# A two-layer decoder on one core: the second token half's FFN pairs multiplied in one pass over both parts of x, and norm factors spread through DRAM

## The chip, the cores and the metric

One NeuronCore of a Trainium2 chip runs the whole kernel. Work is shared by TensorE (PE, matmuls; PEld is its weight load), VectorE (DVE), ScalarE (ACT), GpSimd (POOL) and SyncE (SP, which only issues DMAs). The metric is the device time of one execution in microseconds; a kernel's time is the median of its runs.

## What is computed

512 tokens of 1024 channels go through two layers, all in fp32:

```
layer 0: h += conv_module(rmsnorm(h))        # pointwise+GLU, causal depthwise conv of 31 taps,
                                             # LayerNorm, swish, pointwise
         h += (silu(x@w_gate) * (x@w_up)) @ w_down,   x = rmsnorm(h)     # FFN, inner width 2816
K, V  =  rmsnorm(h) @ w_kv                   # 4 KV heads of 64
layer 1: q = rmsnorm(h) @ w_q                # 16 heads, window of 128 keys, sinks, T5 bias
         h += attention(q, K, V) @ w_o
         h += FFN(rmsnorm(h))
out   =  rmsnorm(h)
rmsnorm(x, g) = x * rsqrt(mean(x*x) + 1e-6) * g
```

## The kernel before, in words

**Layout.** Channels lie on the 128 partitions and tokens along the free axis, so `h` is eight tiles of 128 x 512. A matmul product is 128 x 128 weights (stationary) by 128 x 512 tokens, or by 256 tokens where a half of the tokens is worked on at a time. The convolution module and the first part of layer 0's FFN (inner pairs 0 to 5) run on token half 0, then on token half 1; everything from the second FFN part on runs on all 512 tokens, except the very end, which goes by halves again.

**Split products.** To keep fp32 accuracy, weights and activations are split into a rounded part `hi` (an ACT copy, L203, L382, L386) and a remainder `lo` (a DVE subtraction, L204, L383, L387). `mm3` (L258 to L264) then issues three matmuls for each product into the same sum: `whi` by `xhi` (L262), `whi` by `xlo` (L263) and `wlo` by `xhi` (L264). Each has its own weight load. `Act` (L266) holds the hi and lo parts of an activation in separate tiles of the pool `quads` (11 buffers).

**Weights.** `PLAN` lists every chunk of 512 KB in the order of use. `get` takes the next; `advance` keeps SP loading `raw` tiles up to six chunks ahead (L187, four buffers) and ACT and DVE splitting three chunks ahead (L203, L204; four buffers of each part). An up chunk holds 8 products of 128 x 128 weights, and so does a down chunk.

**FFN.** `ffn_up` works pair by pair (a pair is 256 inner columns): four chunks per pair, two halves of the channels by gate and up. `evac` (L455) takes the sums of a pair out of PSUM: for 256 tokens L461 multiplies the gate by the norm factors on DVE, L463 is Silu, L464 the product with up, L386 and L387 the split into `hid`. There a pair's gate sums share one PSUM bank and its up sums another. `ffn_part` then multiplies `hid` by the down chunks in two groups of four output tiles; L440 and L441 apply the norm factors and add to `h`. For 512 tokens each of a pair's four sums has a bank, and lines L469 to L473 take them out.

**Norms.** `Rms` sums squares: for each tile of `h` a square on ACT (L336) and an addition on POOL (L340). `step1` forms column sums on PE (L350), their mean on DVE (L352), the power -1/2 on POOL (L354) and a diagonal matrix of the factors (on DVE at L357 for 512 tokens, on ACT at L362 for 256). `spread` (L375) multiplies that by ones to bring the factors to all partitions, `step2` copies them to SBUF (L369). `Next.on_h` (L511) issues split (L382, L383) and square for each tile of `h` as it is finished: `n0` and `n1` are the two token halves' norms before layer 0's FFN, and later ones serve K, V and query, and layer 1's FFN. With 256 tokens the first pair calls `step1` at its end, and its sums are taken out in the middle of the second pair.

**The convolution of half 1** runs on DVE (L611), ACT (L603) and POOL (L604) in the background of half 0's matmuls. `job` and `due_at` hand out its steps at points counted in chunks.

**Attention.** A `unit` is four heads by 128 queries, in four stages (`yield` ends one): scores on PE (L927) and bias with maximum on DVE (L930); exponentials on ACT (L937) and the scaling on POOL (L941); transposes on PE (L948) with their split (L951, L952); the product with V on PE (L960) with its split (L966, L967). `pipeline` advances units three, two, one and no steps old, in that order, once per step; 8 units make a pass, two passes are run. The steps are interleaved with the matmuls of the query and the output projection, and `drain` runs what is left of a pass.

**The end.** `Fin` does the last down chunks and the final norm for token half 0 (`fa`), then half 1 (`fb`). `rows` adds to `h` (L1043), squares on ACT (L1047) and sums squares on POOL (L1049); the last squares of half 1 go straight into small matmuls (L1035). `sums` gives the factors (L1066, L1068, L1070), `spread` brings them to a PSUM bank (L1080) and copies that for POOL (L1082). `out_dve` (L1095) makes most output tiles from the bank, `out_pool` (L1089) the others from the copy.

Tile's scheduler orders each engine's instructions from this program order by its own simulation of their times, and adds all waits; `tc.issue_after` pins an order.

Of the kernel before, what the change touches and what calls it, by code (L numbers as in the profile page):

```python
# [149 lines left out]
def hybrid_trunk(ctx: ExitStack, tc: tile.TileContext, xT, W, prm_in, wdw_in, sinks, relb, onehot, outT):  # L150
# [124 lines left out]


# [50 lines left out]
    class Rms:  # L327
        def __init__(self, bc, tok=ALL):
            self.acc = None
            self.bc, self.tok, self.w = bc, tok, tok.stop - tok.start  # L330
            self.eng = nc.gpsimd
            self.stage = 0
# [10 lines left out]
        def step1(self):  # L343
            if self.stage:
                return
            self.stage = 1
            n = self.w // P
            st = bank()
            for i in range(n):
                nc.tensor.matmul(st[:, i:i + 1], self.acc[:, i * P:(i + 1) * P], ones_c, start=i == 0, stop=i == n - 1)  # L350
            ms = small.tile([P, 4], F32, tag="ms", name=uid("ms"))
            nc.vector.tensor_scalar(ms[:, 0:n], st[:, 0:n], 1.0 / D, EPS, op0=ALU.mult, op1=ALU.add)  # L352
            self.rs = small.tile([P, 4], F32, tag="rs", name=uid("rs"))
            nc.gpsimd.tensor_tensor(self.rs[:, 0:n], ms[:, 0:n], mhalf[:, 0:n], op=ALU.pow)  # L354
            self.diag = temp()[:, 0:self.w]
            if n == 4:
                nc.vector.tensor_mul(self.diag.rearrange("p (n q) -> p n q", n=n),  # L357
                                     ident.unsqueeze(1).to_broadcast([P, n, P]),
                                     self.rs.unsqueeze(2).to_broadcast([P, n, P]))
            else:  # L360
                for i in range(n):
                    nc.scalar.mul(self.diag[:, i * P:(i + 1) * P], ident, self.rs[:, i:i + 1])  # L362
# [60 lines left out]
    def ffn_part(layer, part, xg, tok, rms, on_h=None):  # L423
        lo, hi = (HALVES0, HALVES1)[layer][part]
        hid = ffn_up(layer, lo, hi, xg, tok, rms)
        w = tok.stop - tok.start
        for g in range(2):
            if w == 256:
# [22 lines left out]
    def ffn_up(layer, lo, hi, xg, tok, rms):  # L451
        w = tok.stop - tok.start
        hid = Act(2 * (hi - lo), w)

        def evac(pair, banks):  # L455
            rs_bc = rms.step2()
            if w == 256:
# [18 lines left out]
        for pair in range(lo, hi):  # L476
            if w == 256:
# [4 lines left out]
            for half in range(2):  # L482
                for which in range(2):
# [4 lines left out]
                    for k, m in order:  # L488
                        sl = slice(m * P, (m + 1) * P)
                        mm3(banks[which * 2 + m], (whi[:, k, sl], wlo[:, k, sl]), cut(xg[half * 4 + k], tok),  # L490
                            half == 0 and k == 0 and opens(m, w), half == 1 and k == 3 and closes(m, w))
                    if half == 0 and which == 1:
                        if w == 512:
# [4 lines left out]
            if w == 256 and pair == lo:  # L498
# [6 lines left out]
    class Next:  # L505
        def __init__(self, gains, x=None, bc=None, tok=ALL):
            self.gains, self.tok = gains, tok
# [3 lines left out]
        def on_h(self, i):  # L511
            if self.x is None:
                self.x = {self.gains[0]: Act(KT)}
            if self.rms is None:
                self.bc = new_bc() if self.bc is None else self.bc
                self.rms = Rms(self.bc, self.tok)
# [31 lines left out]
    with tc.tile_pool(name="conv", bufs=2) as cv:  # L548
# [275 lines left out]
        x0 = {"ffn0": Act(KT)}  # L824
        bc0 = new_bc()
        n0 = Next(("ffn0",), x0, bc0, HALF[0])
# [19 lines left out]
    ffn_part(0, 0, x0["ffn0"], HALF[1], n1.rms)  # L846
# [11 lines left out]
    if True:  # L858
# [52 lines left out]
        def unit(gp, jp, n):  # L911
# [6 lines left out]
            sc = at.tile([P, 4, 1 + BAND], F32, tag="sc", name=uid("sc"))  # L918
# [21 lines left out]
            for j in range(4):  # L940
                nc.gpsimd.tensor_scalar(sc[:, j, 1:1 + w], sc[:, j, 1:1 + w], sm[:, j:j + 1], 0.0,  # L941
                                        op0=ALU.mult, op1=ALU.add)
            yield
# [72 lines left out]
    class Fin:  # L1016
        def __init__(self, hf):
            self.hf, self.tok = hf, HALF[hf]
            self.banks, self.hg = [bank() for _ in range(4)], []
            self.n_pool = 2 + hf  # L1020
# [17 lines left out]
        def rows(self, g, other=lambda n, ins: None):  # L1038

            n_add = 4 if self.hf else KT  # L1040
            for i in range(g * 4, g * 4 + 4):
# [5 lines left out]
                nc.scalar.square(sq, t)  # L1047
# [30 lines left out]
        def spread(self):  # L1078
            self.pb = bank()[:, 0:256]
            nc.tensor.matmul(self.pb, ones_m, self.diag, start=True, stop=True)  # L1080
            self.bc = temp()[:, 0:256]
            nc.scalar.copy(self.bc, self.pb)  # L1082
# [32 lines left out]
    for n, (kp, g) in enumerate(steps):  # L1115
# [6 lines left out]
        elif n == 3:  # L1122
            fb.rows(1, fill)
    fa.out_pool()
# [31 lines left out]
```

## Time and profile before

| | |
|---|---|
| timed runs | 1122.11, 1123.65, 1123.83 us; median 1123.65 |
| profiled execution | 1122.53 us, span 1120.7 us, granted clock 0.994 |
| PE busy | 1103.7 us (98%), 6140 matmuls |
| DVE, ACT, POOL busy | 663.5 (59%), 509.2 (45%), 324.0 us (29%) |
| DMA | 128.16 MB, 114 GB/s on average |

The stages of the span, by the stretches used below: to about 150 us the convolution module; 150 to 285 the first FFN part on token half 0, with the convolution of half 1 behind it; to 302 half 1's second pointwise product; to 407 the first FFN part on half 1; to 570 the second FFN part; to 594 K and V; to 724 query, attention and the first output products; from about 757 layer 1's FFN; from 1100 the end.

A row of a stretch has: length, then for PE, PEld, DVE, ACT and POOL the busy time and the count, then PE's granted clock, the DMA share and GB/s. A row of a timeline has start, duration, engine, line, operation, tiles and count, and in brackets how long the engine had been idle and what ended that. A row of groups has busy time and mean duration in ns, then idle time before. A row of waits has who waited for whom: us in total, times, the longest. A row of DMA issues ends in the us from issue to landing. Matmul durations overlap, so the pitch of a stream is read from starts.

### The profile page before, as it was taken

The page shows a single profiled execution, that of the slowest core. Times are in us where ns is not written, and L with a number is a line of the kernel's source. Part 1 is how long each engine was busy: PE and PEld are TensorE (multiplying, and loading weights), DVE is VectorE, ACT ScalarE, POOL GpSimd, SP SyncE. Part 2 cuts the span into 40 slices and gives each one's busy share as a digit, 9 for nine tenths or more (in the row PEclk, how much of TensorE's full clock was granted, in tenths as well). Part 3 has the DMA queues.
Part 4 walks back from the last instruction along what each step waited for, and adds up shares of the span by engine and source line. Part 5 has one row for each costly group of instructions (what it writes and reads, how often), then busy time and mean ns, then how long its engine had stood idle before and what let it go on. Part 6 is the DMA issues. An engine that isn't in the chain of part 4 may idle for free.

```text
span 1120.7 us, 16124 instructions
## 1 busy us (share of the span) xinstructions
PE 1103.7 (98%) x6140; PEld 963.7 (86%) x6140; DVE 663.5 (59%) x1072; ACT 509.2 (45%) x898; POOL 324.0 (29%) x425
## 2 busy tenths in 40 slices
PE   9999998999999999999999999999999999999997
PEld 8888888999999998888888777888888888888886
DVE  4999996977756544533575585674443433444455
ACT  3887787746544322323343564553332211232233
POOL 3999699810200001211230232241111100110014
PEclk9999999999999999999999999999999999999998
DMA  9227054585555542233232111123323232333322
GB/s 357 103 31 83 28 179 133 166 266 177 182 180 181 185 151 95 93 113 94 94 94 93 59 38 39 38 76 98 100 87 110 94 94 94 99 103 100 94 94 76
DMA packets 41722, 128.16 MB, mean 114 GB/s; under 512 B 4491, under 2 KB 12844, under 8 KB 41644
## 3 DMA queue, kind: packets, MB, share of 16 engines
q1 hardware_dynamic: 40924, 126.56, 36.4%
q8 instruction: 48, 0.79, 0.3%
q10 hardware_dynamic: 720, 0.57, 0.2%
q14 instruction: 30, 0.25, 0.1%
HBM read 121.87 MB, written 5.24 MB: 113 GB/s over the span
## 4 chain that ended last, share of the span: by engine, by line
PE 90%; DVE 3%; ACT 3%; issue 2%; POOL 1%; DMA 1%; POOLq 0%; SPq 0%; ACTq 0%; DVEq 0%
PE bank L262 26%; PE bank L263 26%; PE bank L264 25%; PE bank L562 9%; PE bank L927 1%; PE bank L649 1%; PE bank L948 1%; ACT pr L603 1%; POOL pr L604 1%; DVE quad L383 1%; ACT whi L203 1%; DVE wlo L204 0%; DVE bank L611 0%; DVE sc L930 0%; DMA raw<-in_W_dram 0%
## 5 line engine op out<-in xcount | busy, mean ns | idle before, releaser
L263 PE MATMUL bank<-quad,whi 128*128 128x512 f32 (+1 forms) x1584 | 543.6, 343 | 1.7 <-DVE quad L383 1.7
L262 PE MATMUL bank<-quad,whi 128*128 128x512 f32 (+1 forms) x1584 | 543.8, 345 | 0.2
L264 PE MATMUL bank<-quad,wlo 128*128 128x512 f32 (+1 forms) x1584 | 542.9, 343 | 0.0
L204 DVE TENSOR_TENSOR wlo<-raw,whi 128x1024 fp32r<-128x1024 f32 x200 | 269.3, 1347 | 318.2 <-ACT whi L203 310.1
L203 ACT CAST whi<-raw 128x1024 fp32r<-128x1024 f32 x200 | 209.4, 1048 | 355.1 <-PE bank L263 301.2
L263 PEld LDWEIGHTS bank<-quad,whi 128*128 128x128 f32 x1584 | 301.0, 190 | 37.5 <-DVE quad L383 2.8
L262 PEld LDWEIGHTS bank<-quad,whi 128*128 128x128 f32 x1584 | 300.7, 190 | 36.5 <-ACT quad L966 0.6
L264 PEld LDWEIGHTS bank<-quad,wlo 128*128 128x128 f32 x1584 | 300.9, 190 | 34.5 <-DVE wlo L204 0.2
L472 POOL TENSOR_TENSOR tmp<-tmp,tmp 128x512 f32<-128x512 f32 x32 | 45.6, 1425 | 485.1 <-DVE tmp L471 471.5
L604 POOL TENSOR_TENSOR pr<-pr,pr 128x256 f32<-128x256 f32 x208 | 160.5, 822 | 11.0 <-ACT pr L603 11.0
L562 PE MATMUL bank<-quad,w 128*128 128x256 f32 x512 | 114.7, 384 | 0.7 <-DMA w<-in_W_dram 0.7
L611 DVE SCALAR_TENSOR_TENSOR bank<-apad,wdw,bank 128x256 f32<-128x256 f32 x248 | 113.2, 485 | 3.5
L562 PEld LDWEIGHTS bank<-quad,w 128*128 128x128 f32 x512 | 98.5, 193 | 14.9 <-DVE quad L537 0.9
L603 ACT ACTIVATE pr<-apad,wdw 128x256 f32<-128x256 f32 x208 | 99.6, 503 | 23.8 <-POOL pr L604 21.7
L340 POOL TENSOR_TENSOR tmp<-tmp,tmp 128x256 f32<-128x256 f32 (+1 forms) x42 | 45.2, 1076 | 135.2 <-ACT tmp L336 111.1
L470 ACT ACTIVATE tmp<-tmp 128x512 f32<-128x512 f32 x32 | 20.1, 632 | 86.5 <-DVE tmp L469 86.5
L941 POOL TENSOR_SCALAR sc<-sc,sm 128x256 f32<-128x256 f32 (+1 forms) x64 | 30.7, 500 | 86.8 <-DVE sm L939 86.7
L386 ACT CAST quad<-tmp 128x512 fp32r<-128x512 f32 (+1 forms) x48 | 27.8, 584 | 28.9 <-POOL tmp L472 25.0
L471 DVE TENSOR_TENSOR tmp<-bank,rsbc 128x512 f32<-128x512 f32 x32 | 22.1, 691 | 30.1 <-PE bank L264 30.1
L383 DVE SCALAR_TENSOR_TENSOR quad<-h,prm,quad 128x512 fp32r<-128x512 f32 (+1 forms) x40 | 39.4, 1020 | 0.5 <-ACT quad L382 0.4
L937 ACT ACTIVATE sc<-sc,m 128x257 f32<-128x257 f32 (+1 forms) x64 | 30.2, 475 | 15.0 <-DVE m L930 14.8
L387 DVE TENSOR_TENSOR quad<-tmp,quad 128x512 fp32r<-128x512 f32 (+1 forms) x48 | 31.0, 651 | 2.3 <-ACT quad L386 2.3
(137 smaller groups left out, 748.6 us busy)
## 6 DMA issues: line engine op xcount, KB each, us to landing
raw<-in_W_dram SPq DMA_DIRECT2D x208, 512.0 KB, 3.5
w<-in_W_dram SPq DMA_DIRECT2D x15, 512.0 KB, 9.7
fd<-fs SPq DMA_DIRECT2D x1, 3072.0 KB, 33.8
h<-in_xT_dram SPq DMA_DIRECT2D x8, 256.0 KB, 6.3
bias<-fd SPq DMA_DIRECT2D x8, 256.0 KB, 7.2
out_dram<-res SPq DMA_DIRECT2D x13, 128.0 KB, 1.8
w<-in_W_dram SPq DMA_DIRECT2D x2, 256.0 KB, 4.3
out_dram<-res ACTq DMA_DIRECT2D x3, 128.0 KB, 2.4
```

The source lines that it names most:

```text
L203: nc.scalar.copy(hi, r)
L204: lo_engine[0].tensor_sub(lo, r, f32(hi))
L262: nc.tensor.matmul(out, w[0], x[0], start=start, stop=False)
L263: nc.tensor.matmul(out, w[0], x[1], start=False, stop=False)
L264: nc.tensor.matmul(out, w[1], x[0], start=False, stop=stop)
L340: self.eng.tensor_add(sq, self.acc, sq)
L383: nc.vector.scalar_tensor_tensor(dst[1], src, g, f32(dst[0]), op0=ALU.mult, op1=ALU.subtract)
L472: nc.gpsimd.tensor_mul(t2, t1, t2)
L562: mm = nc.tensor.matmul(self.pb[:, w * W2:(w + 1) * W2], w1[ct][:, w, k, :], x[k] if x else xg[k][:, tok], start=k == 0, stop=k == KT - 1)
L603: on_act = nc.scalar.mul(pr, a[:, j:j + W2], tap(j))
L604: on_pool = nc.gpsimd.tensor_add(pr, acc, pr)
L611: on_dve = nc.vector.scalar_tensor_tensor(yt if i == nd - 1 else c, src, tap(i), c if i else self.shift, op0=ALU.mult, op1=ALU.add)
```

## The change

It has five parts.

- **Pairs.** `x0` and half 1's `hid` become `Pairs`: hi and lo parts of a tile lie side by side in one tile. With `twin` (half 1's first FFN part only) `mm2` replaces `mm3`: `whi` by both parts at once, 512 columns into a whole bank (the second half of the bank collects `whi` by `lo`), then `wlo` by `hi`, 256 columns, into the first half. `evac` and `ffn_part` add the two halves of each bank (a copy on ACT, an addition on DVE); products go to POOL. Four banks per pair instead of two. `step1` is called in the middle of the first pair, and that pair's sums are taken out at its end.
- **Norm factors by way of DRAM.** With `by_dma` (`n1` and the two norms for 512 tokens) the factors are written to a DRAM line by SP's queue and read back to all partitions by SP's queue. No diagonal, spread or copy.
- **Norm squares on DVE.** `n0` adds its squares on DVE instead of POOL.
- **Later transposes.** A unit waits one step more between scaling and transposes; score buffers are three.
- **Two spreads.** `fb` spreads its factors into two banks, one for DVE, one for the copy that POOL uses; `fa`'s copy is issued behind `fb`'s last square; `fb` sums five squares on POOL and sends three to PE (four and four before); two tiles of `fb` instead of three go to POOL.

In the diff the first `if twin:` stands in `ffn_part`'s loop over the two groups, the second in `evac`, and the doubled `yield` behind a unit's scaling.

```diff
+    class Pairs:
+        def __init__(self, n, w=512):
+            self.per = 1024 // w
+            self.q = [quads.tile([P, self.per, 2, w], F32R, tag="quad", name=uid("quad")) for _ in range(-(-n // self.per))]
+        def both(self, i):
+            return self.q[i // self.per][:, i % self.per]
+        def __getitem__(self, i):
+            b = self.both(i)
+            return b[:, 0, :], b[:, 1, :]
+
+    def mm2(out, w, x, start, stop):
+        first, second = (w[0], x, out), (w[1], x[:, 0, :], out[:, 0, :])
+        if stop:
+            first, second = second, first
+        nc.tensor.matmul(first[2], first[0], first[1], start=start, stop=False)
+        nc.tensor.matmul(second[2], second[0], second[1], start=False, stop=stop)
...
+            if self.by_dma:
+                line = dpool.tile([1, self.w], F32, tag=uid("line"), name=uid("line"))
+                nc.sync.dma_start(line.rearrange("a (n p) -> p (a n)", p=P), self.rs[:, 0:n])
+                nc.sync.dma_start(self.bc[:, self.tok], line.to_broadcast([P, self.w]))
+                self.stage = 2
+                return
...
+            if twin:
...
+                        mm2(banks[m], (whi[:, k, sl], wlo[:, k, sl]), hid.both(2 * (kp - lo) + k),
+                            kp == lo and k == 0, kp == hi - 1 and k == 1)
+                rs_bc = rms.step2()
+                for m, b in enumerate(banks):
+                    t, hm = temp()[:, 0:w], h[g * 4 + m][:, tok]
+                    nc.scalar.copy(t, b[:, 1, :])
+                    nc.vector.tensor_add(t, b[:, 0, :], t)
+                    nc.gpsimd.tensor_mul(t, t, rs_bc)
+                    nc.vector.tensor_add(hm, hm, t)
+                continue
...
+            if twin:
+                t1, t2 = temp(), temp()
+                for which, t in enumerate((t1, t2)):
+                    for m in range(2):
+                        b = banks[which * 2 + m]
+                        tm = t[:, m * w:(m + 1) * w]
+                        nc.scalar.copy(tm, b[:, 1, :])
+                        nc.vector.tensor_add(tm, b[:, 0, :], tm)
+                t1v, t2v = (t.rearrange("p (a s) -> p a s", a=2) for t in (t1, t2))
+                nc.gpsimd.tensor_mul(t1v, t1v, rs_bc.unsqueeze(1).to_broadcast([P, 2, w]))
+                nc.scalar.activation(t1, t1, AF.Silu)
+                nc.gpsimd.tensor_mul(t2, t1, t2)
+                i = 2 * (pair - lo)
+                q = hid.q[i // 4][:, i % 4:i % 4 + 2]
+                nc.scalar.copy(q[:, :, 0, :], t2v)
+                nc.vector.tensor_sub(q[:, :, 1, :], t2v, f32(q[:, :, 0, :]))
+                return
...
-                        if w == 512:
+                        if w == 512 or twin:
                             rms.step1()
...
-        x0 = {"ffn0": Act(KT)}
+        x0 = {"ffn0": Pairs(KT)}
-        n0 = Next(("ffn0",), x0, bc0, HALF[0])
+        n0 = Next(("ffn0",), x0, bc0, HALF[0], nc.vector, by_dma=False)
...
-    ffn_part(0, 0, x0["ffn0"], HALF[1], n1.rms)
+    ffn_part(0, 0, x0["ffn0"], HALF[1], n1.rms, twin=True)
...
             yield
+            yield
...
-            for t in range(len(units) + 3):
-                for d in (3, 2, 1, 0):
+            for t in range(len(units) + 4):
+                for d in (4, 3, 1, 0):
                     if 0 <= t - d < len(units):
                         next(units[t - d])
+                        if d == 1:
+                            next(units[t - d])
...
-            self.n_pool = 2 + hf
+            self.n_pool = 2
-            n_add = 4 if self.hf else KT
+            n_add = 5 if self.hf else KT
...
             nc.tensor.matmul(self.pb, ones_m, self.diag, start=True, stop=True)
+            if self.hf:
+                pb = bank()[:, 0:256]
+                nc.tensor.matmul(pb, ones_m, self.diag, start=True, stop=True)
+                self.copy(pb)
...
+    with tc.issue_after(fb.squared):
+        fa.copy(fa.pb)
     fa.out_pool()
     fb.sums(fill)
     fb.spread()
```

More of the change, by code (lines that the diff above doesn't have):

```diff
@@ L476, in ffn_up @@
         for pair in range(lo, hi):
-            if w == 256:
+            if twin:
+                full = banks = [bank().rearrange("p (a s) -> p a s", a=2) for _ in range(4)]
+            elif w == 256:
                 full = [bank(), bank()]
@@ L489, in ffn_up @@
                         sl = slice(m * P, (m + 1) * P)
+                        if twin:
+                            mm2(banks[which * 2 + m], (whi[:, k, sl], wlo[:, k, sl]), xg.both(half * 4 + k)[:, :, tok],
+                                half == 0 and k == 0, half == 1 and k == 3)
+                            continue
                         mm3(banks[which * 2 + m], (whi[:, k, sl], wlo[:, k, sl]), cut(xg[half * 4 + k], tok),
@@ L497, in ffn_up @@
                         pending = []
-            if w == 256 and pair == lo:
+            if w == 256 and pair == lo and not twin:
                 rms.step1()
@@ L917, in unit @@
             heads = [gp * 8 + g * 4 + 2 * jp + e for g in range(2) for e in range(2)]
[L918 removed]
+            sc = at.tile([P, 4, 1 + BAND], F32, tag="sc", name=uid("sc"), bufs=3)
             sinks4 = sk.rearrange("p (a g j e) -> p a g j e", a=2, g=2, j=2)[:, gp, :, jp, :]
```

40 lines of the change are left out of this document (22 added, 18 removed).

## Prediction

> **What bounds the kernel now.** I read the page's chain first, then stretches of the span, then pitch of matmuls, then PE's waits.
>
> ```profile
> PE 90%; DVE 3%; ACT 3%; issue 2%; POOL 1%; DMA 1%; POOLq 0%; SPq 0%; ACTq 0%; DVEq 0%
> ```
> ```profile
> 320.00:400.00 80.00, 80.00 (x669) 80.00 (x668) 48.25 (x50) 35.24 (x41) 0.00 (x0) 1.00 0.57 185
> 770.00:1100.00 330.00, 330.00 (x1515) 275.73 (x1514) 143.80 (x153) 96.55 (x119) 34.63 (x26) 1.00 0.30 94
> ```
> ```profile
> 168.00:178.60 10.60, 6.64 (x50) 5.83 (x48) 6.45 (x6) 6.91 (x14) 10.60 (x13) 1.00 0.35 112
> 178.60:183.30 4.70, 4.70 (x27) 4.70 (x28) 1.92 (x3) 3.35 (x6) 4.70 (x6) 0.64 0.51 154
> 656.00:671.00 15.00, 13.02 (x90) 10.51 (x90) 12.06 (x33) 9.70 (x29) 6.76 (x14) 1.00 0.12 37
> 711.00:724.00 13.00, 12.23 (x86) 10.11 (x85) 10.17 (x32) 9.19 (x28) 5.68 (x13) 1.00 0.13 42
> ```
> ```profile
> PE bank L350 <- POOL tmp L340: 3.1, 1, 3.1
> PE bank L263 <- DVE quad L383: 1.7, 4, 0.9
> PE bank L263 <- DVE ptl L952: 1.3, 2, 0.7
> PE bank L262 <- ACT pth L951: 0.6, 1, 0.6
> PE bank L948 <- POOL sc L941: 0.6, 1, 0.6
> ```
>
> TensorE carries 90% of the chain. In the long stretches it is busy every microsecond at clock 1.00 (the first figure of a row is the length, then PE, weight loads, DVE, ACT, POOL, clock), while DVE and ACT have 40% and more to spare. So a matmul taken out there shortens the kernel by its pitch, and work added on DVE, ACT or POOL is free until its queue is late. Outside them TensorE is idle 4.0 us of 168 to 178.6, runs the next 4.7 us at clock 0.64, and idles 2.0 and 0.8 us in the attention's two drains. The waits name who is late. The change touches all these places.
>
> **A. The second half's pairs.** The pitch is the distance between starts:
>
> ```profile
> 339.81 0.28 PE L263 MATMUL bank<-quad,whi 128*128 128x256 f32 x1
> ...
> 345.93 0.28 PE L263 MATMUL bank<-quad,whi 128*128 128x256 f32 x1
> ```
> ```profile
> 469.78 0.39 PE L263 MATMUL bank<-quad,whi 128*128 128x512 f32 x1
> ...
> 475.90 0.39 PE L263 MATMUL bank<-quad,whi 128*128 128x512 f32 x1
> ```
>
> The first pair of rows has 51 steps between them, 120.0 ns each; the second 27, 226.7 ns. Doubling the columns adds 106.7 ns, so about 13.3 ns of each matmul do not depend on columns. The second half's FFN has 6 pairs x 4 chunks x 8 products in up and 2 groups x 6 chunks x 8 in down: 288 products, each of three 256-column matmuls now, one of 512 and one of 256 after. 288 x (3 x 120.0 - 226.7 - 120.0) = **3.8 us**. Not shown is a moving operand in two runs (hi and lo parts lie apart): it could pay the constant twice, and A would be 0. I take 3.8, the pitch of the 512 row.
>
> What it adds: per pair four ACT copies and four DVE additions of 256 from PSUM, the elementwise products moved to POOL. Rows for such work:
>
> ```profile
> L638 DVE TENSOR_TENSOR y<-y,bank 128x256 f32<-128x256 f32 x8 | 3.2, 416 | 1.0 <-POOL y L615 1.0
> L1082 ACT COPY tmp<-bank 128x256 f32<-128x256 f32 x2 | 0.7, 373 | 1.3 <-PE bank L1080 1.3
> L472 POOL TENSOR_TENSOR tmp<-tmp,tmp 128x512 f32<-128x512 f32 x32 | 45.6, 1425 | 485.1 <-DVE tmp L471 471.5
> L203 ACT CAST whi<-raw 128x1024 fp32r<-128x1024 f32 x35 | 36.6, 1047 | 53.1 <-PE bank L263 39.5 <-issue 11.9 <-ACT whi L203 1.0
> ```
>
> 4 x 0.37 = 1.5 us more on ACT and, with two 512 products gone, some 0.3 more on DVE, in a pair of about 11.1 us; POOL gets 2 x 1.43 and has nothing else there. All four PSUM banks of a pair are freed by the copies and additions, without the norm factor, and the next pair has the other four. Cover: casts wait for PE (39.5 us), not PE for casts. Without it the 1.5 us would show in each of six pairs.
>
> The page TensorE: Matmul & The Clock Gate of the Trainium skill ("Back-to-back issue gap") gives an isolated warm matmul its columns at 2.4 per ns plus 2.5 ns; an estimate by that is 288 x 2.5 ns, 0.7 us for A instead of 3.8 and 3.1 us more in the end. The trace disagrees for this stream, with 13.3.
>
> **B. Norm factors by way of DRAM.** For three norms the spread matmul goes (the chain of work in order of time):
>
> ```profile
> 319.63 0.43 PE bank L375 x2
> 588.35 0.86 PE bank L375 x2
> 769.21 0.86 PE bank L375 x2
> ```
>
> 0.43 + 0.86 + 0.86 = **2.1 us**, all in stretches where PE is the bound. Also gone are the diagonal products and copies, off the path. Instead SP issues a write of 256 or 512 single words and a read to 128 partitions, one after the other, and what SP has queued behind waits: the raw weight loads. Rows for their price:
>
> ```profile
> raw<-in_W_dram SPq DMA_DIRECT2D x208, 512.0 KB, 3.5
> out_dram<-res SPq DMA_DIRECT2D x13, 128.0 KB, 1.8
> sk<-in_sinks_dram SPq DMA_DIRECT2D x1, 8.0 KB, 10.9
> L1085 SPq DMA_DIRECT2D out_dram<-res x13: 332/388/446, 1110.5 to 1117.3; - x13
> ```
>
> A landing is thus 1.8 to 10.9 us, an issue 0.4. I take 3.5, the row that shares the queue with steady loads; sk's stood behind the first weights. Where is the factor due? Tightest at K and V:
>
> ```profile
> 582.77 1.96 POOL L354 TENSOR_TENSOR rs<-ms,mhalf 128x4 f32<-128x4 f32 x1 [4.19 <-DVE ms L352]
> 590.65 1.28 DVE L892 TENSOR_TENSOR tmp<-bank,rsbc 128x512 f32<-128x512 f32 x2
> 593.91 1.66 DVE L898 TENSOR_SCALAR tmp<-bank,rs 128x256 f32<-128x256 f32 x4 [0.59 <-PE bank L264]
> ```
>
> Factors stand at 584.7; two hops of 3.5 + 0.4 bring them at 592.5, L892 is done at 593.8, and PE wants its two banks for the query at about 593.8: just nothing lost. At the second half's FFN the sums move from the end of the first pair to its middle. There they meet POOL's additions:
>
> ```profile
> 303.73 3.66 POOL L340 TENSOR_TENSOR tmp<-tmp,tmp 128x256 f32<-128x256 f32 x4 [8.35 <-issue]
> 313.28 0.50 PE L350 MATMUL bank<-ones_c,tmp 128*128 128x1 f32 x4
> ```
>
> The pair begins 96 x 0.12 us before 313.3, its middle falls at 307.5 (0.2 less with A), the last sum is there at 307.4: at most 0.1 us. Then additions, 310.9 for the factor's end on POOL (behind two DVE splits), 318.7 in all partitions; only POOL's product waits, and the Silu behind it on ACT, where casts run two chunks of 2.9 us ahead. SP holds a load for about 4 us; a raw tile is loaded some four chunks before its cast. So 0.
>
> **C. The first half's squares on DVE.**
>
> ```profile
> 167.55 3.58 DVE L383 SCALAR_TENSOR_TENSOR quad<-h,prm,quad 128x256 fp32r<-128x256 f32 x4
> 171.04 1.76 DVE L204 TENSOR_TENSOR wlo<-raw,whi 128x1024 fp32r<-128x1024 f32 x1
> 175.62 1.65 DVE L204 TENSOR_TENSOR wlo<-raw,whi 128x1024 fp32r<-128x1024 f32 x1 [2.81 <-ACT whi L203]
> ```
> ```profile
> 175.46 2.39 POOL L604 TENSOR_TENSOR pr<-pr,pr 128x256 f32<-128x256 f32 x2
> 177.81 0.72 POOL L340 TENSOR_TENSOR tmp<-tmp,tmp 128x256 f32<-128x256 f32 x1
> ```
>
> Seven additions (L340) stand between the convolution's (L604) on POOL; PE waits 3.1 us for the last and then runs 4.7 us at 0.64, which loses 4.7 x 0.36 = 1.7: at most 4.8 to gain. On DVE an addition is 0.42 (L638). DVE is full until 172.8, and up to that PE already waits on its L383. If all seven come first, 2.9 us are given back there; if the scheduler puts them behind, in the 2.8 us hole, none. The clock's 1.7 might stay lost too. Range 0.2 to 4.8; I take **3.0**: the last four in part between the L383s, nearly 2 us given back.
>
> **D. Attention, transposes a step later.** To gain there are at most the 2.0 + 0.8 us idle of the drains. Only POOL's 0.6 lies between exponentials and transposes; DVE's 1.3 and ACT's 0.6 lie between a transpose and its product, a distance that stays. The drain now holds one more unit's transposes and products as filler, but also one step more; were that exposed, another 2.0 would be lost. Range -2.0 to 2.8, I take **0.8**, near the one row that the change addresses.
>
> **E. The end.**
>
> ```profile
> 1109.34 2.44 PE L1035 MATMUL bank<-ones_c,sq 128*128 128x1 f32 x20
> 1112.06 0.71 POOL L1068 TENSOR_TENSOR rs<-ms,mhalf 128x2 f32<-128x2 f32 x1 [0.66 <-DVE ms L1066]
> 1114.94 2.05 DVE L1095 SCALAR_TENSOR_TENSOR res<-h,prm,bank 128x256 f32<-128x256 f32 x5 [0.94 <-ACT tmp L1082]
> ```
>
> Four of 20 small matmuls go: 0.5. DVE no longer waits for the copy: 0.4, spent on a sixth product (0.41). The first half's products, now later, can stand before the factor on POOL: up to 0.5 back. Net **0**, within 0.6.
>
> **Sum.** 3.8 + 2.1 + 3.0 + 0.8 + 0 = 9.7 us. The profiled execution took 1122.5 (span 1120.7 and 1.8 around it): 1112.8. The three timed runs' median lies 1.1 above it; the middle of the four executions is 1123.1, so I forecast **1113.4**.
>
> **Rivals.**
> 1. C is eaten: DVE's additions delay the split tiles as much as POOL delayed the sums, and the clock drops as before. For it: DVE without a gap up to 172.8. Against: the hole behind. 1116.4. Chance 0.14.
> 2. Two runs cost like two matmuls, A is 0: 1117.2. For it: no row shows such an operand; against: a full bank is filled at 226.7 ns everywhere else. Chance 0.05. The Trainium skill's gap rule above is a milder form of it, and would end at about 1116.5.
> 3. The drains grow by a step, D is -2.0: 1116.2. For it: DVE 12.06 of 15.00 busy there. Chance 0.08.
> 4. Slower: the factors land late. With sk's 10.9 instead of 3.5 a pair of hops takes 22.6 us: at K and V the banks are free at 608.6, PE waits 14.7; in the FFN the product starts at 333.5 instead of about 315, Silu holds the casts behind it, and past their 6 us of lead some 12.5 are lost. 1140. With L a landing, the two lose 2L - 7.1 and 2L - 9.3; that passes 9.7 at L = 6.5. For it: words of four bytes, which no row shows, behind 512 KB loads on SP's queue; against: 1.8 for whole outputs at the end. The Trainium skill's page DMA: Bandwidth & Descriptors ("Queues, rings and completion order") says each ring is consumed in order, which speaks for the wait behind loads; the 10.9 of sk agrees. Chance 0.11, of which 0.03 end within 0.2%.
>
> The forecast has 0.62. Its bounds with the unknowns: C at 0.2, D at -2.0 and the end at +0.6 give 1119.6; C at 4.8, D at 2.8 and the end at -0.6 give 1109.0. Range 1109 to 1120; it holds rivals 1 to 3. About 0.2% is what can be told from no change. Faster 0.62 + 0.14 + 0.05 + 0.08 = 0.89, same 0.03, slower 0.08.
>
> **What would show it.** A: a pair of rows 347 ns apart per product, no PE idle between 300 and 400. B: no L375 after the first FFN half; PE gapless after K and V. C: no wait of L350, and clock 1.00 behind it; longer waits on the split would show rival 1. D: less idle in the drains. E: 16 small matmuls, end of the span about 12 us after the last wide matmul as now. Wrong: waits of PE on banks freed by L892, casts behind Silu, landings over 4 us.

## The result, and the profile after

| | median, us | range | runs |
|---|---|---|---|
| before | 1123.10 | 1121.84 to 1123.83 | 7 |
| after | 1126.77 | 1126.14 to 1128.38 | 7 |

The ratio is 1.004, 95% interval 1.0029 to 1.0051: slower by 3.7 us, where 9.7 us less was forecast. The profiled execution after took 1126.4 us, span 1124.6, granted clock 0.99.

Where the time went is read first from TensorE's starts at the same places of both traces. The table gives, for stretches of the span, profiled execution minus that of before, in us; the first column holds the start of the kernel and part C, and differs by up to 1.9 here between kernels that leave C as it was (dma_only against third_only). The other kernels are those of the experiments below.

| kernel | to the LayerNorm spread of half 1 (C) | to K/V's norm sums (A, and the FFN's factors) | to the first score (K/V's factors) | to the last norm's sums (D) | to the last split product (third spread) | to the end (E) |
|---|---|---|---|---|---|---|
| after | +0.33 | +1.18 | **+7.29** | **-4.58** | -0.88 | +0.50 |
| nodma | +0.55 | -2.27 | 0.00 | -4.48 | 0.00 | -0.08 |
| dma_only | +1.39 | +0.83 | +5.57 | -0.04 | -0.88 | -0.27 |
| write_on_act | +1.02 | +0.63 | +4.13 | -4.48 | -0.88 | +0.48 |
| write_runs | +0.79 | -1.91 | -0.84 | -4.53 | -0.88 | +0.50 |
| words_apart | +2.46 | -2.58 | -0.84 | -4.57 | -0.88 | -0.09 |
| third_only | -0.54 | -2.28 | 0.00 | -4.52 | -0.88 | +0.41 |

So one stretch lost 7.3 us, one gained 4.6, and the others moved by about one. The page's chain by engine and PE's waits, after:

```profile
PE 83%; issue 4%; DVE 4%; ACT 3%; DMA 3%; POOL 2%; SPq 0%; POOLq 0%; ACTq 0%; DVEq 0%
```
```profile
PE bank L262 <- DVE tmp L956: 6.0, 1, 6.0
PE bank L263 <- DVE quad L405: 3.2, 3, 1.3
PE bank L295 <- DVE wlo L204: 2.5, 2, 1.5
PE bank L1147 <- DVE tmp L1137: 2.1, 1, 2.1
PE bank L264 <- DVE wlo L204: 1.3, 1, 1.3
```

TensorE's share of the chain fell from 90% to 83%, and DMA's rose from 1% to 3%. The wait for GpSimd's sums (L350 before, L371 now) is gone; the longest is now for L956, the product of K's banks with the norm factors (L892 before). What that product waited for stands in the waits of the other engines, and the hops in the chain of work in order of time (start, length, what):

```profile
DVE tmp L956 <- DMA rsbc<-line: 16.9, 1, 16.9
DVE tmp L527 <- DMA rsbc<-line: 16.0, 1, 16.0
POOL tmp L507 <- DMA rsbc<-line: 13.4, 1, 13.4
```
```profile
312.30 7.27 DMA line<-rs
319.58 5.91 DMA rsbc<-line
...
586.27 10.06 DMA line<-rs
596.35 5.87 DMA rsbc<-line
```

At K and V the write of 512 words takes 10.06 us and the read 5.87. VectorE stands 16.9 us in L956, with the freed banks behind it. The stretch by windows, before, then after (length, PE busy, PEld, DVE, ACT, POOL, clock):

```profile
588.00:604.00 16.00, 16.00 (x94) 13.94 (x94) 9.14 (x15) 6.11 (x10) 0.00 (x0) 1.00 0.23 72
```
```profile
588.00:604.00 16.00, 9.95 (x72) 9.23 (x71) 1.69 (x3) 2.01 (x3) 0.00 (x0) 0.88 0.64 48
604.00:612.00 8.00, 8.00 (x30) 6.43 (x29) 7.27 (x13) 3.67 (x7) 0.00 (x0) 0.82 0.39 117
```

TensorE had 16.00 of 16.00 us and now has 9.95, and after the idle time the clock is granted at 0.82 for a while: the wait costs its 6.0 us and more than one behind it.

In the second half's FFN the same thing hits casts, by the detour the prediction's list of signs named: GpSimd's product waits, ScalarE's Silu waits for it, and the cast of weights that stands behind Silu on ScalarE comes late, so VectorE's split of the weights does too.

```profile
325.62 1.28 POOL L507 TENSOR_TENSOR tmp<-tmp,rsbc 128x512 f32<-128x512 f32 x1 [13.35 <-DMA rsbc<-line]
326.94 0.63 ACT L508 ACTIVATE tmp<-tmp 128x512 f32<-128x512 f32 x1 [9.18 <-POOL tmp L507]
327.47 1.03 ACT L203 CAST whi<-raw 128x1024 fp32r<-128x1024 f32 x1
328.54 1.46 DVE L204 TENSOR_TENSOR wlo<-raw,whi 128x1024 fp32r<-128x1024 f32 x1 [9.53 <-ACT whi L203]
```

The 2.5 us of L295 above, in two waits that end at 330.1 and 337.4 us, are most of the price: against nodma, which lacks only the way by DRAM, the stretch is 3.45 us longer (1.18 + 2.27).

### The profile page after: what moved, and what is told of

Same layout as the page of the kernel before. It is cut to its first block, busy times and chain, and to the rows that moved or that the text cites. A ratio compares the mean times of both kernels' runs of the same rounds, so it can differ in the third digit from the quotient of the medians.

```text
span 1124.6 us, 15613 instructions
## 1 busy us (share of the span) xinstructions
PE 1100.1 (98%) x5844; PEld 947.6 (84%) x5844; DVE 676.2 (60%) x1098; ACT 515.9 (46%) x924; POOL 345.4 (31%) x438
## 4 chain that ended last, share of the span: by engine, by line
PE 83%; issue 4%; DVE 4%; ACT 3%; DMA 3%; POOL 2%; SPq 0%; POOLq 0%; ACTq 0%; DVEq 0%
PE bank L262 21%; PE bank L263 21%; PE bank L264 21%; PE bank L626 8%; PE bank L294 4%; PE bank L295 3%; DMA line<-rs 2%; POOL pr L668 1%; PE bank L991 1%; DMA rsbc<-line 1%; ACT pr L667 1%; PE bank L713 1%; PE bank L1013 1%; DVE quad L405 1%; DVE wlo L204 1%
## 5 line engine op out<-in xcount | busy, mean ns | idle before, releaser
L262 PE MATMUL bank<-quad,whi 128*128 128x512 f32 (+1 forms) x1296 | 462.4, 358 | 6.6 <-DVE tmp L956 6.0
L263 PE MATMUL bank<-quad,whi 128*128 128x512 f32 (+1 forms) x1296 | 463.0, 357 | 3.3 <-DVE quad L405 3.2
L264 PE MATMUL bank<-quad,wlo 128*128 128x512 f32 (+1 forms) x1296 | 462.3, 357 | 1.3 <-DVE wlo L204 1.3
L204 DVE TENSOR_TENSOR wlo<-raw,whi 128x1024 fp32r<-128x1024 f32 x200 | 274.9, 1377 | 288.9 <-ACT whi L203 284.3
L262 PEld LDWEIGHTS bank<-quad,whi 128*128 128x128 f32 x1296 | 246.3, 190 | 42.9 <-DVE tmp L956 6.5
L263 PEld LDWEIGHTS bank<-quad,whi 128*128 128x128 f32 x1296 | 246.6, 190 | 39.1 <-DVE quad L405 4.4
L264 PEld LDWEIGHTS bank<-quad,wlo 128*128 128x128 f32 x1296 | 246.5, 190 | 36.3 <-DVE wlo L204 1.5
L294 PE MATMUL bank<-quad,whi 128*128 128x512 f32 x256 | 91.8, 398 | 0.5 <-ACT whi L203 0.5
L361 POOL TENSOR_TENSOR tmp<-tmp,tmp 128x256 f32<-128x256 f32 (+1 forms) x35 | 38.7, 1106 | 136.9 <-ACT tmp L357 112.8
L295 PE MATMUL bank<-quad,wlo 128*128 128x256 f32 x256 | 72.0, 281 | 2.5 <-DVE wlo L204 2.5
L294 PEld LDWEIGHTS bank<-quad,whi 128*128 128x128 f32 x256 | 48.1, 188 | 11.1 <-ACT whi L203 0.8
L295 PEld LDWEIGHTS bank<-quad,wlo 128*128 128x128 f32 x256 | 48.3, 189 | 4.5 <-DVE wlo L204 3.1
```

The source lines that it names most:

```text
L204: lo_engine[0].tensor_sub(lo, r, f32(hi))
L262: nc.tensor.matmul(out, w[0], x[0], start=start, stop=False)
L263: nc.tensor.matmul(out, w[0], x[1], start=False, stop=False)
L264: nc.tensor.matmul(out, w[1], x[0], start=False, stop=stop)
L294: nc.tensor.matmul(first[2], first[0], first[1], start=start, stop=False)
L295: nc.tensor.matmul(second[2], second[0], second[1], start=False, stop=stop)
```

## The experiments

Theory: the way by DRAM cost some 10 us and hid the gains of the other parts. Rival: the other parts lost too (C eaten, drains longer, two-run operands), and DRAM is only one of several. All ratios are to the kernel before, with 95% intervals.

### Which part costs

**nodma**: the changed kernel without the way by DRAM (L570; the old form of the diagonal comes with it).

```diff
-        def __init__(self, gains, x=None, bc=None, tok=ALL, eng=nc.gpsimd, by_dma=True):
+        def __init__(self, gains, x=None, bc=None, tok=ALL, eng=nc.gpsimd, by_dma=False):
```

> The changed kernel with the three norms spread by the matmul again (diagonal, ones, copy), all else as changed. Theory (the factors arrive late by way of DRAM: two landings of 13 to 16 us in all hold PE 6.0 us before the query, with slow clock behind it, and the casts some 3.9 us in the second half's FFN): the median falls by 7.3 + 3.5, less the 0.9 of the third spread, from 1126.8 to about 1116 to 1117, and no PE wait over 1 us is left in either place. Rival (the second half's evacuation by ACT, DVE and POOL makes the casts late by itself, and the K and V wait belongs to the banks): at least the 3.9 us stay, 1120 or more.

Measured: 1116.23 us, ratio 0.9944 (0.9931 to 0.9958). The way by DRAM costs 10.5 us; all else together gains 6.4.

**dma_only**: the kernel before with the way by DRAM at the same three norms.

```diff
+            if self.by_dma:
+                line = dpool.tile([1, self.w], F32, tag=uid("line"), name=uid("line"))
+                nc.sync.dma_start(line.rearrange("a (n p) -> p (a n)", p=P), self.rs[:, 0:n])
+                nc.sync.dma_start(self.bc[:, self.tok], line.to_broadcast([P, self.w]))
...
```

> The kernel before with nothing but the way through DRAM for the same three norms. Theory of the late factors: PE waits about 6 us before the query again and its clock falls behind it, DVE waits for the factors in the second half's FFN; 2.1 us of spreads are saved; 1128 to 1130. Rival (the late factors hurt only together with the new evacuation and early sums): 1121 to 1122, the 2.1 us saved.

Measured: 1128.05, ratio 1.0049 (1.0036 to 1.0062). Alone it costs 5.4, and 5.1 more beside the other parts: by the table 2.6 of these in the second half's FFN (3.45 against 0.83) and 1.7 at K and V (7.29 against 5.57, where the write took 9.1 us and TensorE's wait 4.8 in place of 6.0).

**attn_only**: the kernel before with part D (third score buffer, later transposes). **sc3_only**: with the buffer alone.

```diff
-            sc = at.tile([P, 4, 1 + BAND], F32, tag="sc", name=uid("sc"))
+            sc = at.tile([P, 4, 1 + BAND], F32, tag="sc", name=uid("sc"), bufs=3)
...
-            for t in range(len(units) + 3):
-                for d in (3, 2, 1, 0):
+            for t in range(len(units) + 4):
+                for d in (4, 3, 1, 0):
...
```

> The kernel before with nothing but the later transposes and the third score buffer. From the two traces the stretch from the first score to layer 1's norm sums is 4.6 us shorter in the changed kernel. Theory (the later transposes did that): 1118 to 1119. Rival (it was given back by the 6 us stall ahead of it, in which DVE and ACT ran ahead): 1122 to 1123.5, as the prediction's 0.8 would have it.

> The kernel before with three score buffers in place of two and nothing else; the transposes stay where they were. Theory: part D's gain (1118.24 against 1122.6 with both) comes from the transposes' later place, which lets ptl and pth be cast under other products: the buffer alone gives 0 to 0.8, 1121.8 to 1122.6. Rival: the third buffer frees the score banks' chain and carries most of it: 1119 or less.

Measured: attn_only 1118.24, ratio 0.9963 (0.995 to 0.9975); sc3_only 1121.92, ratio 0.9997 (0.9989 to 1.0006). The later place of the transposes carries the gain; without the third buffer it was not run. Windows over the attention up to the last norm's sums, before and attn_only:

```profile
619.40:757.20 137.80, 135.00 (x797) 110.58 (x797) 93.01 (x234) 77.10 (x206) 44.87 (x85) 1.00 0.16 50
```
```profile
622.10:755.30 133.20, 131.86 (x797) 110.05 (x797) 92.74 (x234) 76.56 (x206) 46.08 (x84) 1.00 0.17 52
```

Both hold the same 797 matmuls, all at clock 1.00. Idle time fell from 2.80 to 1.34, but busy time fell too, from 135.00 to 131.86. From the starts of all matmuls of the stretch: before, a run of transposes met a run of scores 18 times, at about 0.2 us a change where a step within a run takes about 0.1; now 8 times. All 271 steps among transposes and scores together took 29.7 us and now take 26.0, a wait of 0.6 for GpSimd's scaling among them. And the 12 steps from a transpose to a product of probabilities took 2.16 us, now 0.34: that is where PE waited for probabilities that were not cast yet.

**twin_only**: the kernel before with part A. **twin_attn**: with A and D.

```diff
-    ffn_part(0, 0, x0["ffn0"], HALF[1], n1.rms)
+    ffn_part(0, 0, x0["ffn0"], HALF[1], n1.rms, twin=True)
```

> The kernel before with nothing but the one pass over both parts of x in the second half's FFN (part A); squares, score buffers, transposes, tail and spreads as before. Theory: the pair costs 353.2 ns in place of the 360 of three products, as the changed kernel's trace shows, so 288 pairs give 2.0 us: about 1120.6 against 1122.6, ratio 0.998. Rival 1 (the forecast's own size, 13.3 ns a product): 1118.8. Rival 2 (two runs of one operand cost what two products cost, and the 6.8 ns are noise of a gapless stretch): 1122.6, no difference.

> The kernel before with the one pass (A) and the third score buffer and later transposes (D), none of the rest: no way by DRAM, squares on GpSimd, the tail as before. Theory: the gains add, 2.0 for A and 4.4 for D: 1116.2, the same as the changed kernel without its way by DRAM (1116.23), since squares and tail bring nothing. Rival 1: squares and tail each took something in the changed kernel (a lost 0.6 and 0.5 by stages): 1115. Rival 2: squares or tail brought a gain that the stages hid: 1117.5 or more.

Measured: twin_only 1120.24, ratio 0.9981 (0.9972 to 0.9989), a gain of 2.2; twin_attn 1116.21, ratio 0.9944 (0.9931 to 0.9956). The size is that of the pitch. In the changed kernel, in the last product stream of the second half's FFN:

```profile
395.10 0.40 PE L294 MATMUL bank<-quad,whi 128*128 128x512 f32 x1
395.34 0.28 PE L295 MATMUL bank<-quad,wlo 128*128 128x256 f32 x1
...
404.99 0.40 PE L294 MATMUL bank<-quad,whi 128*128 128x512 f32 x1
```

Between the first and the last row lie 28 pairs: 9.89 / 28 = 353.2 ns a pair, of which the wide one takes some 236 and the narrow one 117. Three products took 360.0. In the up products, where the operand lies in two runs, the pair takes 352.

**sq_dve_only**: the kernel before with n0's additions on VectorE (part C). **sq_mixed**: with the last three on VectorE, behind the last split of x.

```diff
-            self.eng = nc.gpsimd
+            self.eng = eng
```
```diff
+            elif self.mixed and self.n >= 5:
+                self.late.append(sq)
...
+            if self.mixed and self.n == KT:
+                a, b, c = self.late
+                nc.vector.tensor_add(b, a, b)
+                nc.vector.tensor_add(c, b, c)
+                nc.vector.tensor_add(c, self.acc, c)
```

> The kernel before with nothing but the first half's squares added on DVE. Theory (the additions, 0.95 us each beside POOL, stand between the split tiles that PE waits for and give back all that POOL's wait cost): 1122.5 to 1124. The prediction's case (3 us gained): 1120.

> The kernel before with one edit: of the seven additions of n0's squares GpSimd does the first four, VectorE the last three behind the last split of x. Theory: part C gained nothing since VectorE's additions stood between the splits, for which the first products wait; behind the last split they cost no wait there, the sum is there by 176, and the wait of 3.1 us of the sums goes: 1119.5 to 1120.5. Rival: VectorE's next casts are then late by what was saved: 1122 to 1123.

Measured: sq_dve_only 1122.60, ratio 1.0001 (0.9993 to 1.001); sq_mixed 1123.36, ratio 1.0006 (0.9998 to 1.0015). The theory of sq_mixed fell. PE's waits, sq_dve_only and then sq_mixed:

```profile
PE bank L263 <- DVE quad L383: 3.2, 3, 1.3
...
PE bank L264 <- DVE wlo L204: 1.3, 1, 1.3
```
```profile
PE bank L384 <- ACT tmp L371: 2.4, 1, 2.4
PE bank L263 <- DVE quad L392: 2.3, 5, 0.9
...
PE bank L264 <- DVE wlo L204: 0.9, 1, 0.9
```

In both the wait of 3.1 us for the sums is gone. In the first its place is taken by the splits (1.7 before) and a late split of weights; in the second PE is sooner at the spread (L384) and waits there for the diagonal, which ScalarE makes (L371) among the convolution's work.

**tail_only**: the kernel before with part E.

```diff
-            n_add = 4 if self.hf else KT
+            n_add = 5 if self.hf else KT
...
```

> The kernel before with the changed tail alone (part E: one GpSimd product more for half 0, one addition more for half 1, two spreads). Theory: nothing to be told, as forecast: 1122.0 to 1123.2. Rival: the stage from the last split product to the end was 0.5 longer in the changed kernel, and this comes from its tail: 1123.2 or more, ratio 1.0005.

Measured: 1123.44, ratio 1.0001 (0.9991 to 1.0011): nothing to be told.

### What makes the write late

**write_runs**: each partition's factors as one run.

```diff
-                nc.sync.dma_start(line.rearrange("a (n p) -> p (a n)", p=P), self.rs[:, 0:n])
+                nc.sync.dma_start(line.rearrange("a (p n) -> p (a n)", p=P), self.rs[:, 0:n])
```

> The changed kernel with one edit: each partition writes its 2 or 4 factors as one run of 8 or 16 bytes instead of words of 4 bytes; the factors so reach other tokens than their own, the same count of them. Theory 1: the write lands late for its number of words (512 and 256 pieces, 7 to 11 us from issue to the read's issue). With 128 pieces it is 3 to 5 us sooner, the matmul that waited 6.0 us for the region bank waits 1 to 2, and the time is 1121 to 1123. Theory 2: the write stands behind the weights' loads on the same engines, whatever its pieces: 7 to 11 us as before, time 1126.8.

**write_on_act**: the write on ScalarE's queue.

```diff
-                nc.sync.dma_start(line.rearrange("a (n p) -> p (a n)", p=P), self.rs[:, 0:n])
+                nc.scalar.dma_start(line.rearrange("a (n p) -> p (a n)", p=P), self.rs[:, 0:n])
```

> The changed kernel with one edit: the write of the factors goes by ScalarE's queue, the read stays on SP's. Theory 1 (pieces): the write still takes 7 to 11 us, and ScalarE is held while it waits for the factors: 1127 to 1129. Theory 2 (SP's queue with the weights' loads ahead of it): the write lands in about 2 to 4 us, the wait of 6.0 us falls to 1 or none: 1120 to 1122.

Measured: write_runs **1116.19**, ratio 0.9941 (0.9928 to 0.9955), 10.6 us less than the changed kernel by its bytes' order alone. write_on_act 1123.64, ratio 1.0013 (1.0004 to 1.0022): the time lies between the two expectations, the landings are those of the first; its writes took 7.1, 8.4 and 8.9 us from issue to the read's issue, against 7.3, 10.1 and 11.4. So the words matter most, and the queue is worth 3.1 us of the time. SP's issues around K and V, after and write_runs:

```profile
586.27 0.38 SPq L378 DMA_DIRECT2D line<-rs  x1
586.74 0.46 SPq L187 DMA_DIRECT2D raw<-in_W_dram  x1
596.35 0.33 SPq L379 DMA_DIRECT2D rsbc<-line  x1
```
```profile
583.64 0.33 SPq L378 DMA_DIRECT2D line<-rs  x1
584.06 0.38 SPq L187 DMA_DIRECT2D raw<-in_W_dram  x1
585.05 0.33 SPq L379 DMA_DIRECT2D rsbc<-line  x1
```

The read is issued when the write has landed: 10.1 us after it in words, 1.4 in runs of 16 bytes, with the same load issued between. At the second half's FFN (256 words, or runs of 8 bytes) it was 7.3 and 3.3.

**words_twice**: the same words written once more, ahead. **words_apart**: as many words, 64 bytes apart, into lines that hold ones.

```diff
+                other = dpool.tile([1, self.w], F32, tag=uid("line"), name=uid("other"))
+                for dst in (other, line):
+                    nc.sync.dma_start(dst.rearrange("a (n p) -> p (a n)", p=P), self.rs[:, 0:n])
```
```diff
+                line = lines.pop()
+                nc.sync.dma_start(line[:, 0:16 * self.w].rearrange("a (n p s) -> p (a n) s", p=P, s=16)[:, :, 0], self.rs[:, 0:n])
+                nc.sync.dma_start(self.bc[:, self.tok], line[:, 0:self.w].to_broadcast([P, self.w]))
```

> The changed kernel with one edit: ahead of each write of the factors the same words are written once more, to a line that nobody reads. Theory: a write of 512 words takes its 10 us on the queue by the number of its words, and two take it one after the other: at K and V the read comes some 8 to 10 us later and all of it falls on TensorE's wait (6.0 to 14 or more); with what the second half's FFN and the last norm lose the time is 1135 to 1150. Rival: the 10 us are a delay of one small write, whatever its words, and two writes run side by side: 1126.8 to 1129.

> The changed kernel with one edit: the same number of four-byte words is written, but 64 bytes apart, into a line that held ones; the read takes the line's first 512 words as before, so most tokens are scaled by one in place of their factor. Theory: the write is late because neighbouring words fall on the same piece of DRAM and follow one another there; apart they land like the runs did, in 1.4 to 3.3 us, and the time is 1116 to 1118. Rival: a word of four bytes is late by itself, wherever it goes: the write takes 7 to 11 us again, 1126 to 1128.

Measured: words_twice 1126.69, ratio 1.0038 (1.0024 to 1.0052), with 7.05, 9.39 and 9.1 us from the second write to the read: the theory that the words' count fills a queue fell. words_apart **1114.14**, ratio 0.992 (0.9906 to 0.9933). SP's issues in it:

```profile
584.64 0.38 SPq L378 DMA_DIRECT2D line<-rs  x1
585.11 0.46 SPq L187 DMA_DIRECT2D raw<-in_W_dram  x1
586.59 0.33 SPq L379 DMA_DIRECT2D rsbc<-line  x1
```

512 words of four bytes land in 1.95 us when they lie apart. Neither their number nor their size is slow, but their closeness: words next to each other in DRAM, coming from different partitions. Two lines side by side do not add up, which agrees.

The single DMA packets kept in the traces show where the time lies. At K and V the last four-byte packet ends 1.3 us after the issue, in the changed kernel as in words_apart. The landing comes 8.8 us after that in the changed kernel and 0.7 in words_apart, and a packet of the load that is queued behind takes up to 10.6 us in the first and at most 0.8 in the second. So the loads ahead did not hold the write back on SP's queue; the close words held up what came behind on the same queue. On ScalarE's queue the words went out later, up to 3.3 us after the issue, and the landing came 5.1 us after the last of them. What goes on in the memory no profile shows, and distances between 4 and 64 bytes were not tried, nor a read of words that lie apart.

### Better versions

**best**: the changed kernel with runs at K/V and the last norm, the spread kept in the second half's FFN, and sq_mixed's additions.

```diff
+                if self.by_dma:
+                    a = self.acc.rearrange("p (q n) -> p n q", n=n)[:, i, :]
...
```

> The changed kernel with three edits: the factors' write for K/V and the last norm goes as one run of 8 or 16 bytes per partition, with the sums matmuls taking every nth token so that each factor stays with its token; the second half's own FFN keeps its spread by TensorE; n0's additions are split as in sq_mixed. Theory: 1116.2 (the changed kernel with such runs), less 0.4 for the spread that was sooner than the read, less up to 3.1 for the squares: 1113 to 1115, below both kernels. Rival: every fourth token as stationary operand loads slowly or the additions make the casts late: 1116 or more.

Measured: 1119.1, ratio 0.9962 (0.995 to 0.9974): the rival. In this kernel V's columns are scaled by factors of other tokens, since they take them from the small tile directly. The sums with every fourth token as weights, and the sums of write_runs with neighbouring tokens; then the windows behind them, in the same order:

```profile
580.74 1.80 PE L383 MATMUL bank<-ones_c,tmp 128*128 128x1 f32 x8
```
```profile
580.43 0.95 PE L371 MATMUL bank<-ones_c,tmp 128*128 128x1 f32 x8
```
```profile
582.00:588.00 6.00, 6.00 (x37) 6.00 (x37) 1.30 (x2) 0.00 (x0) 1.94 (x1) 0.72 0.70 110
```
```profile
582.00:588.00 6.00, 6.00 (x52) 6.00 (x51) 0.74 (x1) 0.68 (x1) 1.62 (x1) 1.00 0.75 179
```

Eight sums take 1.80 us in place of 0.95; at the last norm they are as slow, and that stretch is 0.8 us longer than in write_runs. Behind the sums at K and V the clock is 0.72: 37 matmuls in 6 us instead of 52. That this comes from the slow sums is not shown, and two traces speak against it: behind the same slow sums at the last norm the clock stays at full speed, and attn_only, whose sums read neighbouring tokens, has the same fall in the same place:

```profile
582.00:588.00 6.00, 6.00 (x37) 5.84 (x36) 3.44 (x5) 1.04 (x1) 1.96 (x1) 0.72 0.42 140
```

In both the clock is at half for 3.4 us, worth an estimated 1.7. Of the 2.9 us between best and write_runs the slow sums, used twice, thus explain some 1.7.

**third_only**: the way by DRAM, words and all, at the last norm alone; n0's additions on GpSimd.

```diff
-        nxt = Next(("ffn1",))
+        nxt = Next(("ffn1",), by_dma=True)
```

> The changed kernel, words of four bytes included, with the way by DRAM only at the last norm, where the landing of 11.4 us stood under TensorE's products; the other two norms keep their spread, and n0's squares are added on GpSimd as before. Theory: there the way pays 0.9, the stage from the norm's sums to the last split product is 0.88 shorter than before: 1115.3 against 1116.2 for the changed kernel without the way by DRAM. Rival: the late factor shows in Silu and the casts behind it: 1116.5 or more.

Measured: **1115.72**, ratio 0.994 (0.9927 to 0.9952), with nodma and twin_attn the shortest of the kernels that compute the whole reference; the 0.5 between them is within their ranges, but the stretch itself is 0.88 shorter. The factors are just as late there:

```profile
ACT tmp L533 <- DVE tmp L532: 98.0, 32, 9.8
DVE tmp L532 <- DMA rsbc<-line: 15.5, 1, 15.5
```

VectorE stands 15.5 us, ScalarE 9.8, and no wait of PE follows.

## Why the prediction was wrong, point by point

1. **B, the step that failed.** "I take 3.5, the row that shares the queue with steady loads." The write took 7.3, 10.1 and 11.4 us and the read 5.9 where it is on the chain. The row was near by queue and far by shape: it fills SBUF with 512 KB, this leaves neighbouring words in DRAM. Rival 4 had the mechanism and the sizes: with the two hops of K and V (10.06 + 5.87 for its 2L) its 2L - 7.1 gives 8.8, and the table shows 7.3 lost, 8.1 against write_runs; with 7.27 + 5.91 its 2L - 9.3 gives 3.9, and the table shows 3.1 against write_runs. Its reason for it, four-byte words, was right, though only beside each other; its other reason, the loads ahead on SP's queue, was not: at K and V the last four-byte packet ended 1.3 us after the issue. The Trainium skill's page DMA: Bandwidth & Descriptors ("Queues, rings and completion order"), which was given for the latter, tells of each ring's order; write_on_act, on another queue, took 7.1 to 8.9 us all the same. Its chance of 0.11 was too small: the prediction named a row of 10.9 and one of 1.8 as bounds and then weighed by the middle one.
2. **B's gain** of 2.1 was right for a quick write. In words_apart the three places give -0.31 (against nodma), -0.84 and -0.88, 2.0 in all, and its time is 2.1 less than nodma's. In write_runs they give +0.36, -0.84 and -0.88; its write in the FFN took 3.3 us, and TensorE waits 0.3 there for a split of weights.
3. **A, mis-sized**: 2.2 measured for 3.8. The forecast took 120.0 and 226.7 ns from pure streams; in the mixed stream the pair takes 352 to 353.2, not 346.7, so 7 to 8 ns a product are saved and not 13.3. The operand in two runs costs nothing extra: rival 2 is out. By the Trainium skill's gap rule quoted in the prediction (TensorE: Matmul & The Clock Gate, "Back-to-back issue gap") A would have been 0.7; the runs lie between.
4. **C, wrong**: 3.0 forecast, none measured; rival 1 was right, with a second wait it did not name. After, on VectorE and by windows over the same stretches as in the prediction:

```profile
167.87 0.94 DVE L405 SCALAR_TENSOR_TENSOR quad<-h,prm,quad 128x256 fp32r<-128x256 f32 x1
168.73 0.95 DVE L361 TENSOR_TENSOR tmp<-tmp,tmp 128x256 f32<-128x256 f32 x1
169.61 1.81 DVE L405 SCALAR_TENSOR_TENSOR quad<-h,prm,quad 128x256 fp32r<-128x256 f32 x2
```
```profile
168.00:178.60 10.60, 8.64 (x45) 8.14 (x46) 10.16 (x10) 7.45 (x15) 10.60 (x11) 0.68 0.22 61
178.60:183.30 4.70, 4.70 (x42) 4.70 (x41) 2.32 (x3) 4.28 (x7) 4.70 (x7) 1.00 0.72 214
```

   An addition (L361) takes 0.95 us between the splits, not the 0.42 of the row that was used. PE idles 2.0 us instead of 4.0, but the low clock has moved ahead: 0.68 over these 8.64 us costs an estimated 2.8, where 0.64 over 4.7 cost 1.7. A wait of 1.3 at 204.7 us for a split of weights takes the rest. By the traces' record of the clock it is at half for 6.8 us here, and for 3.4 before. All seven kernels with these additions on VectorE show 6.8. Of the eight with all of them on GpSimd five show 3.4 and three 6.8 (dma_only, tail_only, twin_only), so part of what this stretch shows belongs to the single execution; the medians of sq_dve_only and sq_mixed do not rest on it.
5. **D, mis-sized**: 4.4 measured for 0.8. The bound "at most the 2.0 + 0.8 us idle of the drains" looked at idle time alone; two thirds of the gain (3.1 of 4.6) is busy time. The 10 fewer changes between transposes and scores, 0.2 us each in place of 0.1, make an estimated 1.0 of it; what makes the rest is not shown.
6. **E**: none, as forecast.

By parts: A +2.2, D +4.4, C and E none, so 1116.2 without the way by DRAM; that way then cost 10.5 where 2.1 were to be gained.

## What to carry to other kernels

Price a DMA by a row with the same shape of pieces at its destination, and where there is none, let the chance follow the bounds and not the middle. Neighbouring words from many partitions into one line of DRAM land late; give each partition a run (which here needs sums over every fourth token to keep each factor with its own, at 0.85 us a time), or use such a way only where the result is due late: write and read together took 13 to 16 us here. For a change in an engine's order, look at how its busy time is spent too (how often it changes between kinds of work), not at its idle time alone.

## What the runs showed that was not expected

- 512 words of four bytes next to each other in DRAM land in 8.4 to 11.4 us, 64 bytes apart in 1.95 to 2.1, and as 128 runs of 16 bytes in 1.4 (once, in best, 3.1). A second such write ahead of it adds nothing. Packets of the load behind the close words take up to 10.6 us each.
- The same addition on VectorE, 128x256 from SBUF, takes 0.95 us beside GpSimd's convolution products, and 0.77 to 0.78 for the last of the chain (sq_mixed, the changed kernel).
- Weights loaded from every fourth token make eight narrow sums 0.85 us longer.
- A spell at half clock near n0's sums lasts 3.4 us in some kernels and 6.8 in others whose code there is the same; behind K and V's sums attn_only has one of 3.4 and the kernel before has none.
